# A last gate tile made in two token parts, and a shorter reciprocal root

## The chip, the core and the metric

The kernel runs on one core of a Trainium2 chip. The metric is device time in microseconds (us): the median of several runs, beside one profiled execution whose trace shows every instruction. TensorE multiplies matrices (in the profile PE, its weight loads PEld), VectorE (DVE) and ScalarE (ACT) do elementwise work, GpSimd (POOL) and SyncE (SP) mostly start transfers.

## What is computed

One inference step of a hybrid decoder trunk with one layer: 256 prompt tokens and 8 samples of 4 tokens, 288 tokens in all, of width 2048. The part that matters here is the end of the layer and the norm that is used throughout:

```python
def rmsnorm(x, g):
    xf = x.astype(jnp.float32)
    y = xf * lax.rsqrt(jnp.mean(xf * xf, axis=-1, keepdims=True) + EPS)
    return (y * g.astype(jnp.float32)).astype(x.dtype)
...
    gate = jax.nn.sigmoid(rmsnorm(h, g_pg) @ w_pg)
    h = h + (p_l @ w_ple) * gate
...
    y_prompt = rmsnorm(hp, g_final)
    y_sample = rmsnorm(hs, g_final)
```

Ahead of that stand a combined input projection, a state-space head group, a gated spatial mixing group, an output projection and a feed-forward block, all joined by such norms.

## The kernel before, in words

Activations lie transposed: the 2048 channels are 16 tiles of 128 partitions, and the 288 tokens run along the free dimension. A projection makes one output tile of 128 channels at a time: `mtile` loads two halves of 512 KB of weights on SyncE's queue, `split_w` cuts each into a rounded part (`whi`, ScalarE, L177) and a rest (`wlo`, VectorE, L178), and `mm3` (L184 to L186) multiplies each of 16 blocks three times (hi by hi, hi by lo, lo by hi) in the fp32r type. So an output tile is 48 matmuls with 288 columns each, and every matmul has its own weight load. The splits are given a higher priority than the work around them; otherwise the framework orders each engine's instructions from the program's order and a simulated timeline.

A norm needs one number for each token. `sum_tokens` (L109) sums squares over partitions by three matmuls against a column of ones, each of which shows as two passes; it gives a tile of 128 partitions and 3 columns, one column for tokens 0 to 127, one for 128 to 255 and one for the last 128 (of which only the last 32 tokens are needed). `rsqrt_compact` (L76) turns it into reciprocal roots on VectorE: x, a first guess by integer arithmetic on the bits, three Newton steps. `bcast_tokens` (L121) brings the result back to all partitions by two transposes (L125) and one small matmul (L126). There are eight such norms: `rm` before the first projection, `rg` four times, `rv`, `rf`, `rp`, and `ro` at the end.

The last stage is the loop over 16 output tiles of the gate projection (`w_pg`). For each tile, VectorE multiplies by the norm (L835), ScalarE takes a tanh (L836), VectorE adds and multiplies with the embedding (L837) and adds to `h` (L838), ScalarE squares (`no.add`, L146), VectorE adds to the running sum `sacc` (L147), and ScalarE scales `h` by the final gain (L846). The chain of one tile runs under the matmuls of the next. For the last tile these steps are made in two halves of 128 and 160 tokens, the sums of the tiles ahead are taken early (`part`, L845, six passes between the last matmuls), and the last tile's squares are summed by themselves. After the root and the broadcast, VectorE multiplies `h` in nine pieces of one or two tiles (L851), each followed by its store (L852) on ScalarE's or SyncE's queue in turn.

Of the kernel before, what the change touches and what calls it, by code (L numbers as in the profile page):

```python
# [10 lines left out]
F32 = mybir.dt.float32  # L11
F32R = mybir.dt.float32r
I32 = mybir.dt.int32
AF = mybir.ActivationFunctionType
ALU = mybir.AluOpType
PSUM = bass.MemoryType.PSUM

P = 128
NT = 288
KD = 16  # L20
EPS = 1e-6
# [8 lines left out]
V_MIX, V_FFN, V_PG, V_FIN, V_SSD, V_CM, V_DSK, V_CB, V_CW = 0, 16, 32, 48, 64, 80, 96, 112, 136  # L30
# [10 lines left out]
def hybrid_step(ctx: ExitStack, tc: tile.TileContext, xT, wa, wd, wple, pT, vec, cst, wdt, dtal,  # L41
                sconv, h0T, wsT, wsS, bsP, bsS,
                o_y, o_ssmp, o_conv, o_ssms, o_v):
    nc = tc.nc
# [4 lines left out]
    pa = ctx.enter_context(tc.tile_pool(name="pacc", bufs=3, space=PSUM))  # L49
    pb = ctx.enter_context(tc.tile_pool(name="pbig", bufs=5, space=PSUM))  # L50

    def slab(dt=F32, name="slab", tag="slab"):
        return sp.tile([P, NT], dt, tag=tag, name=name, bufs=SLOTS[tag])

    def big(name="pb"):
        return pb.tile([P, 512], F32, tag="pb", name=name)

    def small(shape, name, bufs=1, dt=F32):
        return cp.tile(shape, dt, tag=name, name=name, bufs=bufs)
# [9 lines left out]
    def bc_mid(ap, n):  # L69

        return ap.unsqueeze(1).to_broadcast([ap.shape[0], n, ap.shape[1]])

    def f32(ap):
        return ap.bitcast(F32)

    def rsqrt_compact(ss, n, eps, name, part=None):  # L76

        x = small([P, 3], name + "x")
        y = small([P, 3], name + "y")
        t = small([P, 3], name + "t")  # L80
        if part is None:
            nc.vector.tensor_scalar(x, ss, 1.0 / n, eps, op0=ALU.mult, op1=ALU.add)
        else:
            nc.vector.scalar_tensor_tensor(x, ss, 1.0 / n, part, op0=ALU.mult, op1=ALU.add)
        nc.vector.tensor_scalar(t.bitcast(I32), x.bitcast(I32), 1, None, op0=ALU.logical_shift_right)  # L85
        nc.vector.tensor_scalar(y.bitcast(I32), t.bitcast(I32), -1, 0x5F3759DF, op0=ALU.mult, op1=ALU.add)  # L86
        for _ in range(3):
            nc.vector.tensor_mul(t, y, y)  # L88
            nc.vector.scalar_tensor_tensor(t, t, -0.5, x, op0=ALU.mult, op1=ALU.mult)  # L89
            nc.vector.scalar_tensor_tensor(y, t, 1.5, y, op0=ALU.add, op1=ALU.mult)  # L90
        return y

    def quads(ap):
# [12 lines left out]
    def sum_tokens(ps, acc, first=True, last=True):  # L106

        for c, t in enumerate((0, P, NT - P)):
            nc.tensor.matmul(ps[:, c:c + 1], lhsT=acc[:, t:t + P], rhs=ones[:, 0:1], start=first and c == 0,  # L109
                             stop=last and c == 2)  # L110

    def sum_compact(acc):

        ps = big()
        sum_tokens(ps, acc)
        return ps[:, 0:3]

    def rstd_compact(acc, n, eps, name, part=None):
        return rsqrt_compact(sum_compact(acc), n, eps, name, part)

    def bcast_tokens(r, keep_psum=False):  # L121

        ps = big()
        for c in range(2):
            nc.tensor.transpose(ps[:, c * P:(c + 1) * P], r[:, c:c + 1].to_broadcast([P, P]), ident)  # L125
        nc.tensor.matmul(ps[:, 256:288], lhsT=r[:, 2:3].to_broadcast([P, P]),  # L126
                         rhs=ident[:, 96:128], start=True, stop=True)
        if keep_psum:
            return ps[:, :NT]
        o = slab(name="rs", tag="rs")  # L130
        nc.scalar.copy(o, ps[:, :NT])
        return o
# [34 lines left out]
    def load(src, k):  # L167
        raw = st.tile([P, 1024], F32, tag="raw", name="raw", bufs=4)
        nc.sync.dma_start(raw[:, :k * P], src.rearrange("p k m -> p (k m)"))
        return raw  # L170

    def split_w(raw, n, to=None, ahead=AHEAD):
        w_hi, w_lo = to or [st.tile([P, 1024], F32R, tag=t, name=t) for t in ("whi", "wlo")]
        a, b = w_hi[:, :n * P], w_lo[:, :n * P]
        r = raw[:, :n * P]
        with tc.high_priority(offset=ahead):
            nc.scalar.copy(a, r)  # L177
            nc.vector.tensor_sub(b, r, f32(a))  # L178
        return w_hi, w_lo

    def mm3(ps, w, k, act, first, last):
        hi, lo = act
        wh, wl = w[0][:, k * P:(k + 1) * P], w[1][:, k * P:(k + 1) * P]
        nc.tensor.matmul(ps, lhsT=wh, rhs=hi, start=first, stop=False)  # L184
        nc.tensor.matmul(ps, lhsT=wh, rhs=lo, start=False, stop=False)  # L185
        nc.tensor.matmul(ps, lhsT=wl, rhs=hi, start=False, stop=last)  # L186
# [18 lines left out]
    ones = small([P, P], "ones")  # L205
    T1, U, ident = (csts[:, c:c + P] for c in (C_T1, C_U, C_I))
# [8 lines left out]
    def vcol(base, i):  # L215
        return vecs[:, base + i:base + i + 1]
# [6 lines left out]
    start = tc.tile_pool(name="start", bufs=1)  # L223
# [33 lines left out]
    for c in range(4):  # L257
        w = split_w(wraw[c], 8)
        for j in range(4):
            ps = pa.tile([P, NT], F32, tag="acc", name="acc")  # L260
# [14 lines left out]
    with tc.high_priority(offset=400):  # L275
        rs0 = bcast_tokens(rstd_compact(sqa[:, 0], 2048.0, EPS, "rm"), keep_psum=True)
# [3 lines left out]
    for k in range(KD):  # L280
        nc.tensor.matmul(pdt[32 * (k % 4):32 * (k % 4) + 32, 0:NT], lhsT=gw[:, k], rhs=xin[k // 2][:, k % 2],
                         start=k < 4, stop=k >= 12, tile_position=(0, 32 * (k % 4)))
# [297 lines left out]
    def y_norm_a(g, grp):  # L580
        return g, rstd_compact(grp.acc, 512.0, 4.0 * EPS, "rg")
# [22 lines left out]
    ss = {}  # L604
# [109 lines left out]
    at = 0  # L714
    for g in range(4):
        tiles = [16 + g, 20 + g] + list(range(4 * g, 4 * g + 4))
        zs = []
        for j, i in enumerate(tiles):
            ps = ps01[at] if at < 3 else mtile(wa[at], n_act)
# [31 lines left out]
    hp, h, mlp_pool, mp, sw = hp_box["pools"]  # L751
    for m in range(KD):
        ps = mtile(wa[40 + m], ycat[:16])
        nc.vector.tensor_add(h[:, m], h[:, m], ps)

    for i in range(nvt, KD):
        ps = mtile(wa[56 + i], n_act)
# [3 lines left out]
    for i in range(KD):  # L761
        ps = mtile(wa[72 + i], n_act)
        us.append(gelu2(ps, hp.tile([P, NT], F32, tag="u", name="u", bufs=4))[0])
        advance(1)
        while us and ss and i - len(us) + 1 in ss:
            k = i - len(us) + 1
# [12 lines left out]
    for m in range(KD):  # L779
        ps = mtile(wa[88 + m], ycat[16:])  # L780
# [6 lines left out]
    g_act = []  # L787
    rs = None
    for half in range(2):
        hid = []  # L790
        for m in range(22):
            mm = 22 * half + m
            pg = mtile(wa[104 + 2 * mm], f_act)
            pu = None
            if rs is None:
                r = rstd_compact(nf.acc, 2048.0, EPS, "rf")
                pu = mtile(wa[105 + 2 * mm], f_act)
                rs = bcast_tokens(r)
            G = hp.tile([P, NT], F32, tag="g2", name="G", bufs=3)
            t, u = slab(name="Gt", tag="ta"), slab(name="Up", tag="td")  # L800
            nc.vector.tensor_mul(G, pg, rs)  # L801
            nc.scalar.activation(t, G, AF.Tanh, scale=0.5)  # L802
            nc.vector.scalar_tensor_tensor(G, t, 1.0, G, op0=ALU.add, op1=ALU.mult)  # L803
            if pu is None:
                pu = mtile(wa[105 + 2 * mm], f_act)
            nc.vector.scalar_tensor_tensor(u, pu, 0.5, rs, op0=ALU.mult, op1=ALU.mult)  # L806
            nc.vector.tensor_mul(u, u, G)  # L807
            hid.append(split(u, make=extra if m >= 18 else None))
        for m in range(KD):
            ps = mtile(wd[half, m], hid)  # L810
            nc.vector.tensor_add(h[:, m], h[:, m], ps)  # L811
            if half == 1:
                g_act.append(split(h[:, m], gain=vcol(V_PG, m), tags=LONG))
                ng.add(h[:, m])
                if m == 7:
                    ple = fp.tile([P, KD, NT], F32, name="ple", bufs=1)
# [3 lines left out]

    no = SumSq()
    wait, rs = [], None
    for m in range(KD):
        wait.append(mtile(wa[192 + m], g_act))
        if m == 0:
            r = rstd_compact(ng.acc, 2048.0, EPS, "rp")
            continue
        if rs is None:
            rs = bcast_tokens(r)
        for k in range(m + 1 - len(wait), m + 1):  # L830
            ps = wait.pop(0)
            G = hp.tile([P, NT], F32, tag="g2", name="G", bufs=3)

            for c in (slice(0, NT),) if k < KD - 1 else (slice(0, P), slice(P, NT)):
                nc.vector.tensor_mul(G[:, c], ps[:, c], rs[:, c])  # L835
                nc.scalar.activation(G[:, c], G[:, c], AF.Tanh, scale=0.5)  # L836
                nc.vector.scalar_tensor_tensor(G[:, c], G[:, c], 1.0, ple[:, k, c], op0=ALU.add, op1=ALU.mult)  # L837
                nc.vector.scalar_tensor_tensor(h[:, k, c], G[:, c], 0.5, h[:, k, c], op0=ALU.mult, op1=ALU.add)  # L838
                if k == KD - 1:
                    nc.scalar.activation(G[:, c], h[:, k, c], AF.Square)  # L840
            if k < KD - 1:
                no.add(h[:, k], scratch=G)
                if k == KD - 2:
                    part = small([P, 3], "part")
                    nc.vector.tensor_scalar(part, sum_compact(no.acc), 1.0 / 2048.0, EPS, op0=ALU.mult, op1=ALU.add)  # L845
            nc.scalar.activation(h[:, k], h[:, k], AF.Identity, scale=vcol(V_FIN, k))  # L846
    rs = bcast_tokens(rstd_compact(G, 2048.0, EPS, "ro", part), keep_psum=True)
    at = 0
    for i, n in enumerate((1, 1, 2, 2, 2, 2, 2, 2, 2)):
        hq = h[:, at:at + n]  # L850
        nc.vector.tensor_mul(hq, hq, bc_mid(rs, n))  # L851
        (nc.sync if i % 2 else nc.scalar).dma_start(o_y[:, at:at + n], hq)  # L852
        at += n


def _consts():
# [104 lines left out]
```

## Time and profile before

| | us |
|---|---|
| median of three runs | 1747.91 (1745.03 to 1748.62) |
| the profiled execution, its own time | 1745.97 |
| its span in the trace | 1744.2 |
| TensorE's mean granted clock in it | 0.991 of full speed |

The page of the profile gives for each engine the busy time and its share of the span. Rows of groups give line, engine, operation, output and inputs, shapes, count, then busy us and mean ns of one. Rows of the timeline give start, length, engine, line and operation; where neighbouring instructions of a group are merged, the count is behind the `x`, and the length is from the first start to the last end. In brackets stands the idle time before, and what ended it. Ends of matmuls are modelled, so the distance between starts says more than the length.

### The profile page before, as it was taken

What the parts mean: (1) busy time and instruction counts of PE and PEld (TensorE: products, weight loads), DVE (VectorE), ACT (ScalarE), POOL (GpSimd) and SP (SyncE); (2) the same over time, 40 slices, a digit from 0 to 9 for tenths busy, and PEclk for the clock granted to TensorE, in tenths of its full rate; (3) what the DMA queues carried; (4) which work ended last, traced back from release to release, by engine and by line L of the source; (5) the groups of instructions that cost most, each with busy time, mean ns of one, the idle gap of its engine ahead of it and who ended that gap; (6) DMA issues with size and microseconds to landing.
All of it is one profiled execution on the core that took longest, in us unless ns stands there. A gap on an engine that the chain in (4) does not pass through costs nothing.

```text
span 1744.2 us, 31331 instructions
## 1 busy us (share of the span) xinstructions
PE 1712.5 (98%) x12920; PEld 1686.5 (97%) x12920; DVE 1067.0 (61%) x1680; ACT 806.3 (46%) x1354; POOL 40.5 (2%) x100
## 2 busy tenths in 40 slices
PE   7999999999999999999999999999999999999996
PEld 6989999989999999999999999999999999999996
DVE  6778888775455876555555554444555555555665
ACT  5677676643356444443333333333333333344453
POOL 2001011010000000000000000000000000000000
PEclk8999999999999999999999999999999999999998
DMA  8447375665555446555455455555555555555552
GB/s 309 165 142 285 128 272 190 222 253 173 164 166 169 153 136 219 171 163 164 164 164 168 160 168 157 167 166 175 162 166 164 164 169 159 163 166 166 170 167 93
DMA packets 86240, 307.00 MB, mean 176 GB/s; under 512 B 9969, under 2 KB 10481, under 8 KB 85329
## 3 DMA queue, kind: packets, MB, share of 16 engines
q1 hardware_dynamic: 77760, 275.07, 48.5%
q0 software_dynamic: 7616, 28.60, 4.3%
q8 instruction: 101, 1.65, 0.4%
q10 hardware_dynamic: 720, 1.33, 0.2%
q14 instruction: 43, 0.34, 0.1%
HBM read 290.18 MB, written 14.79 MB: 175 GB/s over the span
## 4 chain that ended last, share of the span: by engine, by line
PE 76%; DVE 0%; issue 0%; DVEq 0%
PE acc L184 25%; PE acc L186 25%; PE acc L185 25%; PE pb L643 0%; DVE h L851 0%; PE pb L635 0%; PE pb L109 0%; PE pb L125 0%; PE pb L126 0%; DVE rot L89 0%; DVE rot L88 0%; DVE roy L90 0%; DVEq L950 0%; DVE rot L85 0%; DVE roy L86 0%
## 5 line engine op out<-in xcount | busy, mean ns | idle before, releaser
L184 PE MATMUL acc<-hi,whi 128*128 128x288 f32 x4032 | 1195.5, 297 | 5.9 <-ACT whi L177 5.9
L186 PE MATMUL acc<-hi,wlo 128*128 128x288 f32 x4032 | 1189.4, 295 | 3.5 <-DVE wlo L178 3.3
L185 PE MATMUL acc<-lo,whi 128*128 128x288 f32 x4032 | 1191.1, 295 | 0.0
L177 ACT CAST whi<-raw 128x1024 fp32r<-128x1024 f32 (+1 forms) x516 | 534.2, 1036 | 820.3 <-PE acc L185 635.9
L178 DVE TENSOR_TENSOR wlo<-raw,whi 128x1024 fp32r<-128x1024 f32 (+1 forms) x516 | 622.7, 1208 | 469.1 <-ACT whi L177 464.5
L186 PEld LDWEIGHTS acc<-hi,wlo 128*128 128x128 f32 x4032 | 760.0, 189 | 9.1 <-DVE wlo L178 5.4
L184 PEld LDWEIGHTS acc<-hi,whi 128*128 128x128 f32 x4032 | 757.7, 188 | 11.2 <-ACT whi L177 7.0
L185 PEld LDWEIGHTS acc<-lo,whi 128*128 128x128 f32 x4032 | 758.9, 188 | 1.5 <-issue 1.3
L806 DVE SCALAR_TENSOR_TENSOR Up<-acc,rs 128x288 f32<-128x288 f32 x44 | 20.1, 457 | 42.2 <-PE acc L186 42.2
L801 DVE TENSOR_TENSOR G<-acc,rs 128x288 f32<-128x288 f32 x44 | 20.1, 457 | 41.6 <-PE acc L186 41.6
L382 DVE SCALAR_TENSOR_TENSOR cva<-cbuf,cwh,cva 128x312 f32<-128x312 f32 x72 | 38.4, 536 | 0.5
L597 ACT ACTIVATE gt<-gt 128x288 f32<-128x288 f32 x32 | 14.2, 443 | 40.6 <-DVE gt L596 40.6
L429 ACT ACTIVATE xw<-xdt,dec 128x64 f32<-128x64 f32 x96 | 24.7, 338 | 5.2 <-DVE xdt L426 5.1
L411 ACT ACTIVATE M<-cq,cum 128x128 f32<-128x128 f32 x64 | 19.9, 389 | 7.3 <-DMA cq<-cdram 7.2
L460 DVE TENSOR_TENSOR h<-h,pb 128x512 f32<-128x512 f32 x32 | 20.4, 682 | 2.9 <-PE pb L458 2.8
L807 DVE TENSOR_TENSOR Up<-Up,G 128x288 f32<-128x288 f32 x44 | 20.2, 459 | 1.5
L467 DVE TENSOR_TENSOR h<-h,decS 128x512 f32<-128x512 f32 x32 | 20.1, 684 | 0.5 <-PE pb L533 0.5
L803 DVE SCALAR_TENSOR_TENSOR G<-Gt,G 128x288 f32<-128x288 f32 x44 | 19.9, 453 | 0.1
L802 ACT ACTIVATE Gt<-G 128x288 f32<-128x288 f32 x44 | 19.2, 437 | 1.4 <-DVE G L801 1.4
L163 DVE TENSOR_TENSOR lo<-Up,hi 128x288 fp32r<-128x288 f32 x44 | 19.9, 451 | 0.0
L162 ACT CAST hi<-Up 128x288 fp32r<-128x288 f32 x44 | 19.1, 433 | 1.3 <-DVE Up L807 0.5
L811 DVE TENSOR_TENSOR h<-h,acc 128x288 f32<-128x288 f32 x32 | 14.5, 455 | 6.0 <-PE acc L186 6.0
(269 smaller groups left out, 786.4 us busy)
## 6 DMA issues: line engine op xcount, KB each, us to landing
raw<-in_wa_dram SPq DMA_DIRECT2D x416, 512.0 KB, 3.6
raw<-in_wd_dram SPq DMA_DIRECT2D x64, 512.0 KB, 3.5
raw<-in_wd_dram SPq DMA_DIRECT2D x32, 384.0 KB, 3.1
h<-in_h0T_dram POOLq DMA_DIRECT2D x16, 512.0 KB, 8.0
out_dram<-h POOLq DMA_DIRECT2D x16, 512.0 KB, 5.5
cq<-cdram SPq DMA_DIRECT2D x4, 1152.0 KB, 7.3
xin<-in_xT_dram SPq DMA_DIRECT2D x8, 288.0 KB, 6.8
pdram<-ple POOLq DMA_DIRECT2D x16, 144.0 KB, 4.7
```

The source lines that it names most:

```text
L177: nc.scalar.copy(a, r)
L178: nc.vector.tensor_sub(b, r, f32(a))
L184: nc.tensor.matmul(ps, lhsT=wh, rhs=hi, start=first, stop=False)
L185: nc.tensor.matmul(ps, lhsT=wh, rhs=lo, start=False, stop=False)
L186: nc.tensor.matmul(ps, lhsT=wl, rhs=hi, start=False, stop=last)
L382: nc.vector.scalar_tensor_tensor(ao, cb[:, j:j + NCO], wt[j], ao, op0=ALU.mult, op1=ALU.add)
L429: nc.scalar.activation(xw[:, 64 * h:64 * h + 64], xd[:, 64 * h:64 * h + 64], AF.Identity, scale=dec[:, c, 8 * g + h:8 * g + h + 1])
L460: nc.vector.tensor_add(h0[q][:, i], h0[q][:, i], pss[q])
L467: nc.vector.tensor_mul(r3(hh, 64), r3(hh, 64), bc_in(decS[:, 2 * q + i, hs], 64))
L801: nc.vector.tensor_mul(G, pg, rs)
L806: nc.vector.scalar_tensor_tensor(u, pu, 0.5, rs, op0=ALU.mult, op1=ALU.mult)
L807: nc.vector.tensor_mul(u, u, G)
```

## The change

`rsqrt_compact` takes a tile of any width. The first guess takes one instruction instead of two (the halving and the subtraction from the constant are made as one multiplication and addition on the integer value). The three Newton steps become one third-order step of four instructions and one Newton step of three. For a width of one, where x and y are scalars of each partition, both products of a step are one instruction, and the last factor is returned to the caller instead of being multiplied in.

The loop over the gate's tiles stops ahead of the last. The last tile's weights are loaded and split once, and its matmuls are made in two parts, first for tokens 0 to 127, then for 128 to 287, each into its own accumulator: 96 matmuls of 128 or 160 columns instead of 48 of 288. After 11 of the second part's 16 blocks TensorE takes the first part's sums (running sum and the last tile's squares together, one column). The first part's root, broadcast, multiplies and stores come beside the second part: half of them behind the second part's gate, half behind the second part's root. The second part's outputs then go in five pieces of 1, 3, 4, 4 and 4 tiles. `tc.issue_after` puts an engine's instructions behind the one named. `part` is gone.

```diff
-    def rsqrt_compact(ss, n, eps, name, part=None):
-
-        x = small([P, 3], name + "x")
-        y = small([P, 3], name + "y")
-        t = small([P, 3], name + "t")
-        if part is None:
-            nc.vector.tensor_scalar(x, ss, 1.0 / n, eps, op0=ALU.mult, op1=ALU.add)
-        else:
-            nc.vector.scalar_tensor_tensor(x, ss, 1.0 / n, part, op0=ALU.mult, op1=ALU.add)
-        nc.vector.tensor_scalar(t.bitcast(I32), x.bitcast(I32), 1, None, op0=ALU.logical_shift_right)
-        nc.vector.tensor_scalar(y.bitcast(I32), t.bitcast(I32), -1, 0x5F3759DF, op0=ALU.mult, op1=ALU.add)
-        for _ in range(3):
-            nc.vector.tensor_mul(t, y, y)
-            nc.vector.scalar_tensor_tensor(t, t, -0.5, x, op0=ALU.mult, op1=ALU.mult)
-            nc.vector.scalar_tensor_tensor(y, t, 1.5, y, op0=ALU.add, op1=ALU.mult)
+    def rsqrt_compact(ss, n, eps, name):
+
+        w = ss.shape[1]
+        x = small([P, w], name + "x")
+        y = small([P, w], name + "y")
+        t = small([P, w], name + "t")
+        nc.vector.tensor_scalar(x, ss, 1.0 / n, eps, op0=ALU.mult, op1=ALU.add)
+        nc.vector.tensor_scalar(y.bitcast(I32), x.bitcast(I32), -0.5, float(0x5F3759DF), op0=ALU.mult, op1=ALU.add)
+
+        def residual():
+            if w == 1:
+                nc.vector.tensor_scalar(t, y, y, x, op0=ALU.mult, op1=ALU.mult)
+            else:
+                nc.vector.tensor_mul(t, y, y)
+                nc.vector.tensor_mul(t, t, x)
+
+
+        residual()
+        nc.vector.scalar_tensor_tensor(t, t, -10.0 / 3.0, t, op0=ALU.add, op1=ALU.mult)
+        nc.vector.scalar_tensor_tensor(y, t, 5.0, y, op0=ALU.add, op1=ALU.mult)
+        a = -0.5 * (3.0 / 8.0) ** 3
+        if w == 1:
+            residual()
+            nc.vector.tensor_scalar(y, t, 1.5 * 3.0 / 8.0 / a, y, op0=ALU.add, op1=ALU.mult)
+            return y, a
+        nc.vector.tensor_mul(t, y, y)
+        nc.vector.scalar_tensor_tensor(t, t, a, x, op0=ALU.mult, op1=ALU.mult)
+        marks["rsqrt"] = nc.vector.scalar_tensor_tensor(y, t, 1.5 * 3.0 / 8.0, y, op0=ALU.add, op1=ALU.mult)
         return y
...
-    for m in range(KD):
+
+    def gated(k, ps, rs, c, no=None):
+
+        G = hp.tile([P, NT], F32, tag="g2", name="G", bufs=3)
+        nc.vector.tensor_mul(G[:, c], ps[:, c], rs[:, c])
+        nc.scalar.activation(G[:, c], G[:, c], AF.Tanh, scale=0.5)
+        nc.vector.scalar_tensor_tensor(G[:, c], G[:, c], 1.0, ple[:, k, c], op0=ALU.add, op1=ALU.mult)
+        marks["gated"] = nc.vector.scalar_tensor_tensor(h[:, k, c], G[:, c], 0.5, h[:, k, c],
+                                                        op0=ALU.mult, op1=ALU.add)
+        if no is None:
+            nc.scalar.activation(G[:, c], h[:, k, c], AF.Square)
+        else:
+            no.add(h[:, k], scratch=G)
+        nc.scalar.activation(h[:, k, c], h[:, k, c], AF.Identity, scale=vcol(V_FIN, k))
+        return G
+
+    for m in range(KD - 1):
...
-    rs = bcast_tokens(rstd_compact(G, 2048.0, EPS, "ro", part), keep_psum=True)
-    at = 0
-    for i, n in enumerate((1, 1, 2, 2, 2, 2, 2, 2, 2)):
-        hq = h[:, at:at + n]
-        nc.vector.tensor_mul(hq, hq, bc_mid(rs, n))
-        (nc.sync if i % 2 else nc.scalar).dma_start(o_y[:, at:at + n], hq)
-        at += n
+            gated(k, wait.pop(0), rs, slice(0, NT), no)
+
+
+    k = KD - 1
+    w = [split_w(load(wa[192 + k, :, 8 * i:8 * i + 8], 8), 8) for i in range(2)]
+    parts = [slice(0, P), slice(P, NT)]
+    pss = [pa.tile([P, NT], F32, tag="acc", name="acc") for _ in parts]
+    sums = [big() for _ in parts]
+
+    def products(j, ks):
+        c = parts[j]
+        for i in ks:
+            mm3(pss[j][:, c], w[i // 8], i % 8, [x[:, c] for x in g_act[i]], i == 0, i == KD - 1)
+
+    def final_sums(j, G):
+        cols = (0,) if j == 0 else (P, NT - P)
+        for x in (no.acc, G):
+            for i, t in enumerate(cols):
+                mm = nc.tensor.matmul(sums[j][:, i:i + 1], lhsT=x[:, t:t + P], rhs=ones[:, 0:1],
+                                      start=x is no.acc and i == 0, stop=x is G and i == len(cols) - 1)
+        return mm
+
+    def final_rstd(j):
+
+        ro = big()
+        if j == 0:
+            r, scale = rsqrt_compact(sums[j][:, 0:1], 2048.0, EPS, "roa")
+            nc.tensor.transpose(ro[:, 0:P], r.to_broadcast([P, P]), ident)
+            return ro[:, 0:P], scale
+        r = rsqrt_compact(sums[j][:, 0:2], 2048.0, EPS, "rob")
+        nc.tensor.transpose(ro[:, 0:P], r[:, 0:1].to_broadcast([P, P]), ident)
+        nc.tensor.matmul(ro[:, P:160], lhsT=r[:, 1:2].to_broadcast([P, P]), rhs=ident[:, 96:128],
+                         start=True, stop=True)
+        return ro[:, 0:160], None
+
+    def put(j, ro, scale, ns, at=0):
+        for i, m in enumerate(ns):
+            hq = h[:, at:at + m, parts[j]]
+            if scale is None:
+                nc.vector.tensor_mul(hq, hq, bc_mid(ro, m))
+            else:
+                nc.vector.scalar_tensor_tensor(hq, hq, scale, bc_mid(ro, m), op0=ALU.mult, op1=ALU.mult)
+            (nc.sync if j == 0 or i % 2 else nc.scalar).dma_start(o_y[:, at:at + m, parts[j]], hq)
+            at += m
+
+    products(0, range(KD))
+    products(1, range(11))
+    summed = final_sums(0, gated(k, pss[0], rs, parts[0]))
+    with tc.issue_after(summed.ins):
+        products(1, range(11, KD))
+    G = gated(k, pss[1], rs, parts[1])
+    first = final_rstd(0)
+    with tc.issue_after(marks["gated"].ins):
+        put(0, *first, (4, 4))
+    final_sums(1, G)
+    second = final_rstd(1)
+    with tc.issue_after(marks["rsqrt"].ins):
+        put(0, *first, (4, 4), 8)
+    put(1, *second, (1, 3, 4, 4, 4))
```

More of the change, by code (lines that the diff above doesn't have):

```diff
@@ L74, in f32 @@
         return ap.bitcast(F32)
-    def rsqrt_compact(ss, n, eps, name, part=None):
-        x = small([P, 3], name + "x")
-        y = small([P, 3], name + "y")
-        t = small([P, 3], name + "t")
-        if part is None:
-            nc.vector.tensor_scalar(x, ss, 1.0 / n, eps, op0=ALU.mult, op1=ALU.add)
-        else:
-            nc.vector.scalar_tensor_tensor(x, ss, 1.0 / n, part, op0=ALU.mult, op1=ALU.add)
-        nc.vector.tensor_scalar(t.bitcast(I32), x.bitcast(I32), 1, None, op0=ALU.logical_shift_right)
-        nc.vector.tensor_scalar(y.bitcast(I32), t.bitcast(I32), -1, 0x5F3759DF, op0=ALU.mult, op1=ALU.add)
-        for _ in range(3):
-            nc.vector.tensor_mul(t, y, y)
-            nc.vector.scalar_tensor_tensor(t, t, -0.5, x, op0=ALU.mult, op1=ALU.mult)
-            nc.vector.scalar_tensor_tensor(y, t, 1.5, y, op0=ALU.add, op1=ALU.mult)
+    marks = {}
+    def rsqrt_compact(ss, n, eps, name):
[22 more added lines that the diff above has]
+        marks["rsqrt"] = nc.vector.scalar_tensor_tensor(y, t, 1.5 * 3.0 / 8.0, y, op0=ALU.add, op1=ALU.mult)
         return y
@@ L116, in sum_compact, with rstd_compact @@
         return ps[:, 0:3]
-    def rstd_compact(acc, n, eps, name, part=None):
-        return rsqrt_compact(sum_compact(acc), n, eps, name, part)
+    def rstd_compact(acc, n, eps, name):
+        return rsqrt_compact(sum_compact(acc), n, eps, name)
     def bcast_tokens(r, keep_psum=False):
@@ L830, in hybrid_step @@
         for k in range(m + 1 - len(wait), m + 1):
[L831 to L846, printed above, removed]
-    rs = bcast_tokens(rstd_compact(G, 2048.0, EPS, "ro", part), keep_psum=True)
-    at = 0
-    for i, n in enumerate((1, 1, 2, 2, 2, 2, 2, 2, 2)):
-        hq = h[:, at:at + n]
-        nc.vector.tensor_mul(hq, hq, bc_mid(rs, n))
-        (nc.sync if i % 2 else nc.scalar).dma_start(o_y[:, at:at + n], hq)
-        at += n
+            gated(k, wait.pop(0), rs, slice(0, NT), no)
```

## The prediction

> **What bounds the kernel now.** I read the page of the profile first, for the share of each engine, then TensorE's waits, then the timeline of the last 23 us.
>
> ```profile
> span 1744.2 us, 31331 instructions
> PE 1712.5 (98%) x12920; PEld 1686.5 (97%) x12920; DVE 1067.0 (61%) x1680; ACT 806.3 (46%) x1354; POOL 40.5 (2%) x100
> ```
>
> TensorE works for 98% of the span. A change can shorten the run only if TensorE gets less to do, or where TensorE waits, or after its last instruction. The list of its waits shows where it idles on a reciprocal root:
>
> ```profile
> PE pb L125 <- DVE rmy L90: 3.4, 1, 3.4
> PE pb L125 <- DVE roy L90: 2.5, 1, 2.5
> PE pb L109 <- issue: 1.9, 1, 1.9
> ```
>
> Of the eight calls of the root, only the first (`rm`, before the first projection) and the last (`ro`, at the end) hold TensorE up. The other six, four `rg` and `rv`, `rf`, `rp`, are in no row of the list: shortening them is worth nothing, and the cover is the matmul stream that runs meanwhile. The third row is the wait for the last tile's gate and square. The timeline of the end, in which PE is TensorE, DVE VectorE and ACTq a DMA issue on ScalarE's queue:
>
> ```profile
> 1721.47 0.29 PE L184 MATMUL acc<-hi,whi 128*128 128x288 f32 x1
> ...
> 1727.34 0.29 PE L186 MATMUL acc<-hi,wlo 128*128 128x288 f32 x1
> 1727.47 0.72 PE L109 MATMUL pb<-ones,sacc 128*128 128x1 f32 x6
> 1728.06 0.38 PE L184 MATMUL acc<-hi,whi 128*128 128x288 f32 x1
> ...
> 1728.27 0.30 PE L185 MATMUL acc<-lo,whi 128*128 128x288 f32 x1
> 1728.41 0.29 PE L186 MATMUL acc<-hi,wlo 128*128 128x288 f32 x1
> 1728.74 0.52 DVE L835 TENSOR_TENSOR G<-acc,rs 128x128 f32<-128x128 f32 x2 [0.35 <-PE acc L186]
> ...
> 1730.22 0.57 ACT L840 ACTIVATE G<-h 128x128 f32<-128x128 f32 x2 [0.59 <-DVE h L838]
> 1730.63 0.82 PE L109 MATMUL pb<-ones,G 128*128 128x1 f32 x6 [1.93 <-issue]
> 1731.49 0.16 DVE L84 SCALAR_TENSOR_TENSOR rox<-pb,part 128x3 f32<-128x3 f32 x1 [1.06 <-PE pb L109]
> ...
> 1733.66 0.16 DVE L90 SCALAR_TENSOR_TENSOR roy<-rot,roy 128x3 f32<-128x3 f32 x1
> 1733.97 0.66 PE L125 MATMUL pb<-cst,roy 128*128 128x128 f32 x2 [2.51 <-DVE roy L90]
> 1734.42 0.47 PE L126 MATMUL pb<-cst,roy 128*128 128x32 f32 x2
> 1734.93 5.47 DVE L851 TENSOR_TENSOR h<-h,pb 128x288 f32<-128x288 f32 x9 [1.11 <-PE pb L126]
> 1740.43 0.34 ACTq L852 DMA_DIRECT2D out_dram<-h  x1
> ```
>
> The last tile starts at 1721.47 and ends at 1728.41 + 0.29 = 1728.70. From there everything is serial to the end at 1744.20: gate and square to 1730.79, sums to 1731.49, root to 1733.82, broadcast to 1734.93, nine multiplies to 1740.40, then the last store. These 15.5 us are what the change wants to fold into the matmuls. Its price is paid on TensorE, which has no idle time in the last tile.
>
> **The change part by part.** All times are in this profiled execution, whose own time is 1745.97 us: its span of 1744.2 and 1.77 around it.
>
> *Roots.* The chain has 12 instructions before: one for x, two for the first guess, three times three. After it has 9 where w is over 1 (x, guess, four, three) and 7 where w is 1. In `ro` 11 steps lie between the starts at 1731.49 and 1733.66, so a step is 0.197 us and three fewer save 0.59. This counts twice. At the start the chain of `rm` gates this:
>
> ```profile
> 36.45 0.69 PE L125 MATMUL pb<-cst,rmy 128*128 128x128 f32 x2 [3.45 <-DVE rmy L90]
> ...
> 37.34 3.30 PE L281 MATMUL pdt<-xin,gw 128*32 128x288 f32 x32
> 40.56 0.53 PE L184 MATMUL ps<-hi,whi 128*128 128x288 f32 x2
> ```
>
> TensorE goes from the broadcast to the dt matmuls and the first projection without a gap, so all of it moves up: **-0.59**. Late next would be the normalized activations on VectorE, and they start from the same broadcast.
>
> *The last tile's matmuls.* Before, 48 matmuls of 288 columns: from 1721.47 to 1727.34 there are 44 intervals, so one takes 0.133 us and 48 take 6.40. After, there are 96, of 128 and 160 columns, each with its own load of 128x128 weights. No row shows an fp32r matmul below 288 columns. The nearest row with full weight loads and nearly nothing to stream is the six passes of L109 with one column: from 1727.34 to 1728.27 pass one matmul of L186, six passes and one of L184, so a pass takes (0.93 - 0.27)/6 = 0.111. That is the pace of load and issue, and a narrow matmul cannot be paid less than it on this evidence. I take 0.111 for both widths, because by columns alone they would cost less (0.133/288 = 0.463 ns a column, 0.059 and 0.074 us) and so hide under the load. The sums of the running squares shrink from six passes in the tile to four, since the other columns' sums go behind the last matmul. So 7.06 becomes 100 passes x 0.111 = 11.10: **+4.04**. Bounds: by columns alone 48 x 0.133 = 6.4 for both parts, 4.26 less; at the full 0.133 each 2.1 more; at the pace of plain f32 (next fence) 12.9 more.
>
> ```profile
> 594.01 0.61 PE L643 MATMUL pb<-wsr,vt 128*128 128x128 f32 x4
> ...
> L643 PE MATMUL pb<-wsr,vt 128*128 128x128 f32 x64 | 9.6, 274 | 0.0
> ...
> 109.05 1.02 PE L506 MATMUL pb<-xw,btm 128*128 128x512 f32 x2
> ...
> L506 PE MATMUL pb<-xw,btm 128*128 128x512 f32 x8 | 4.1, 593 | 0.0
> ```
>
> A plain f32 matmul shows as two passes. At 128 columns the starts lie (0.61 - 0.274)/3 = 0.112 apart, at 512 columns 1.02 - 0.593 = 0.43, some 0.83 ns a column. Two passes would be 0.224 for 128 columns and 0.267 for 160, together 0.491 x 48 = 23.6.
>
> The Trainium skill, page "TensorE: Matmul & The Clock Gate", section "Back-to-back issue gap", gives about 81 ns for a sustained pair of load and matmul at 128 columns. By it 96 matmuls would be an estimated 7.8 us, and the whole change about 2.2 us faster instead of 0.7 slower. The trace's one-column pairs at 0.111 with f32 weights speak against it here, so the sum goes by the row.
>
> *Gate and square.* Before, two halves through five instructions, 1728.74 to 1730.79, 2.05 us. After the last matmul only the 160 columns are left.
>
> ```profile
> L835 DVE TENSOR_TENSOR G<-acc,rs 128x160 f32<-128x160 f32 x1 | 0.3, 314 | 0.0
> ...
> L840 ACT ACTIVATE G<-h 128x160 f32<-128x160 f32 x1 | 0.3, 336 | 0.0
> ...
> L851 DVE TENSOR_TENSOR h<-h,pb 128x576 f32<-128x576 f32 x7 | 4.7, 747 | 0.0
> L851 DVE TENSOR_TENSOR h<-h,pb 128x288 f32<-128x288 f32 x2 | 0.8, 452 | 1.1 <-PE pb L126 1.1
> ```
>
> Five of 0.31 to 0.34 with four handovers of some 0.03 make 1.75: **-0.30**. The first part's gate runs under the second part's matmuls: it needs some 2 us, the 33 matmuls ahead of its sums take 3.7, so TensorE does not wait.
>
> *First outputs.* Two multiplies of 512 columns sit behind the gate on VectorE, queued ahead of the second root. In the nine multiplies 5.47 = 2 x 0.37 + 6 x 0.664 + 0.747, with 0.37 the step of 288 columns and 0.664 that of 576 (an instruction starts some 0.08 before the one ahead of it ends). At 1.02 ns a column a 512 step is 0.60. From gate to root VectorE had 0.34 + 0.03 + 0.70 = 1.07 free (square, handover, sums); two steps need 1.22, and with a drain I take **+0.2**. The second root saves **-0.59**. Behind it come two more multiplies in the gap of the broadcast, which was 1.11 and shrinks by one transpose: 1.22 against 1.11, **+0.15**. If the first root were not done by then, this would cost more (a rival, below).
>
> *Second outputs.* Widths 160, 480 and three of 640: 0.24 + 0.57 + 2 x 0.73 + 0.81 = 3.08 instead of 5.47: **-2.39**.
>
> *Stores.* They shrink to rows of 512 and 640 bytes from 2304, in 9 DMAs as before, four of them early. SyncE's queue carries the early ones; nothing else waits in it.
>
> ```profile
> out_dram<-h ACTq DMA_DIRECT2D x4, 288.0 KB, 2.3
> ...
> DMA packets 1211, 2.27 MB, mean 391 GB/s; under 512 B 128, under 2 KB 327, under 8 KB 1211
> ```
>
> From 1736.5 to 1742.3 the stores move 2.27 MB at 391 GB/s, so they run at VectorE's pace. The second part, 1.31 MB in 3.08 us, asks for 425 GB/s: **+0.2** of backlog. No row shows short rows at speed. If they cost nothing the term is 0; at 240 GB/s, six tenths of the row, it is about +2.4.
>
> The Trainium skill, page "DMA: Bandwidth & Descriptors", section "Why small descriptors are slow (HBM only)", counts about 3 cycles for each packet beside its 32-byte beats. By it rows of 640 bytes run at an estimated 0.87 of the wire and 2304 at 0.96, which would make the term some 0.6; no run here shows it.
>
> Sum: -0.59 + 4.04 - 0.30 + 0.20 - 0.59 + 0.15 - 2.39 + 0.20 = **+0.7 us**, so 1746.7 for this execution. The median of the runs shown is 1747.91, 1.94 above it, and the same step gives **1748.6**.
>
> **The rivals.** *Narrow matmuls at f32's pace.* In the last tile a narrow fp32r matmul takes the two-pass time, 0.224 and 0.267. For it: every fp32r matmul in the trace has 288 or more columns, and all narrow ones are f32. Against it: each fp32r matmul of the last tile is one instruction, and nothing shows a dependence on width. The sum becomes +13.6, 1761.5: clearly slower. It decides once the mean interval passes 0.140, where the sum reaches 3.5.
>
> *Narrow matmuls paid by columns.* If the loads overlapped fully, 0.059 and 0.074 would give -3.5, 1744.4. For it: TensorE's loads run beside its matmuls, 97% of the span beside 98%. Against it: 0.111 for one column. The same page of the Trainium skill states in its section "Step-by-step: what each phase is for" that throughput is purely the number of columns streamed; the L109 rows do not agree where the stream is one column.
>
> *The first root is late.* If VectorE gets the seven instructions of the first root behind the second gate, 7 x 0.197 + about 1.0 for the broadcast stand ahead of the first outputs and thus of the second root: +2.4, total +3.1, 1751.0. For it: the program writes it in that order. Against it: VectorE's order in the trace follows readiness (the weight splits run ahead of earlier lines), and its inputs are ready 1.7 us of matmuls earlier.
>
> **How the numbers follow.** A measurement of this kernel tells a difference of about 0.2%, 3.5 us, from none. Load-bound matmuls (+0.7; alone from 1747.5 to 1752.0, by 0.133 a pair or slow stores): 0.60. F32's pace: 0.18. By columns: 0.12. Late first root: 0.10. Faster by over 0.2% takes about two thirds of the third case and little else, 0.09. Slower takes the second, four tenths of the fourth and a tenth of the first, 0.28. The rest, 0.63, is the same. The range must reach f32's pace, or more than 2 in 10 would be left out, and it leaves out most of the third case: 1745.0 to 1762.0.
>
> **What would show it.** In the changed profile: narrow matmuls starting 0.11 apart, and the last tile taking 11 us with its four sums; if 0.06 to 0.08 or over 0.2, that term failed. Second root 9 steps of 0.2; first multiply of the second part about 1.3 us behind it; from the last matmul to the end about 12.8 us instead of 15.5. The first projection matmul near 40.0 instead of 40.56. Seven instructions of the first root under the second part's matmuls, not behind its gate. Stores well below 390 GB/s at the end would show short rows.

## The result, and the profile after

The changed kernel takes 1737.98 us (median of 4 runs, 1737.12 to 1739.04) against 1747.53 (1745.03 to 1748.62) for the kernel before on the same chip: ratio 0.9946, 95% interval 0.9934 to 0.9957. It is some 9.5 us faster, where +0.7 was forecast. The profiled execution took 1737.12, so its trace can stand beside that of before (1745.97). The head of its page:

```profile
span 1735.3 us, 31405 instructions
PE 1710.4 (99%) x12968; PEld 1686.8 (97%) x12968; DVE 1064.6 (61%) x1659; ACT 806.1 (46%) x1355; POOL 40.4 (2%) x100
```

TensorE is busy 2.1 us less than before (1712.5), though the last tile has 48 more matmuls. The span is 8.9 us shorter, so most of the gain is idle time that went. To find where, I number the projection matmuls (those of `mm3`) in order of start and take, for the n-th, its start in the trace of before minus its start in the trace of another kernel. This lead, in us, for all kernels of this study, each in its profiled execution (the experiments follow):

| kernel | n = 100 | 400 | 700 | 2220 | 2340 | 12000 |
|---|---|---|---|---|---|---|
| changed kernel | 1.73 | 1.72 | 3.40 | 3.71 | 11.27 | 11.25 |
| all new roots, old last tile | 0.37 | 0.35 | 2.02 | 2.35 | 9.91 | 9.90 |
| old roots, new last tile | -0.36 | -0.37 | -0.77 | -1.64 | -3.14 | -3.16 |
| new root in `rg` alone | 0.16 | 0.15 | -0.13 | -0.40 | 7.14 | 7.16 |
| new root in `rm` alone | 1.17 | 1.15 | 2.82 | 4.24 | 2.92 | 2.91 |
| new root in the last `rg` alone | 0.09 | 0.09 | 0.26 | -0.19 | 2.73 | 2.71 |
| old roots, mask later | -0.48 | -0.50 | -0.79 | -0.46 | 2.71 | 3.03 |
| old roots, `rg` of higher priority | 0.69 | 0.69 | 0.53 | 0.91 | 4.09 | 4.09 |
| changed kernel, long store rows | 0.49 | 0.39 | 2.06 | 2.38 | 9.91 | 9.89 |
| new roots in `rm` and `rg` | 1.50 | 1.50 | 3.17 | 3.49 | 11.03 | 11.05 |

The first row tells three things. The lead is made at three places: before the first projection, between matmuls 400 and 700 (1.68), and above all between 2220 and 2340 (7.56), which in before run from 380 to 404 us. From there it stays, to the last tile. The column n = 100 differs from one execution to the next: two kernels that were profiled twice show 1.73 and 1.00 (the changed one), 0.37 and 1.88 (all new roots, old last tile). Their steps between 2220 and 2340 agree to 0.02. And the last tile, which the change is about, adds nothing to it: from its first matmul to the end of the span it takes 1735.3 - 1710.22 = 25.08 us after and 1744.20 - 1721.47 = 22.73 before, so it loses 2.35.

The windows of before around the big step (columns: length, then busy time of PE, PEld, DVE, ACT and POOL with counts, TensorE's granted clock, DMA share, GB/s):

```profile
385.00:390.00 5.00, 3.63 (x26) 3.13 (x25) 3.25 (x7) 2.96 (x6) 0.00 (x0) 1.00 1.03 419
390.00:395.00 5.00, 4.55 (x34) 4.31 (x33) 2.11 (x6) 1.26 (x3) 0.00 (x0) 1.00 0.85 355
395.00:400.00 5.00, 2.43 (x9) 1.96 (x10) 5.00 (x5) 1.87 (x2) 0.00 (x0) 0.81 0.15 22
400.00:405.00 5.00, 5.00 (x34) 5.00 (x34) 1.75 (x2) 1.05 (x1) 0.00 (x0) 0.85 0.83 278
```

and of after:

```profile
385.00:390.00 5.00, 5.00 (x40) 5.00 (x39) 4.25 (x6) 2.93 (x3) 0.00 (x0) 1.00 1.01 415
390.00:395.00 5.00, 5.00 (x40) 5.00 (x40) 3.06 (x3) 1.43 (x2) 0.00 (x0) 1.00 0.80 317
395.00:400.00 5.00, 5.00 (x40) 5.00 (x40) 3.60 (x4) 1.72 (x2) 0.00 (x0) 1.00 0.43 155
```

Before, TensorE is busy for 2.43 of the 5 us from 395, VectorE for all 5; then the clock falls below 1. After, TensorE runs through. The waits of before between 380 and 402 us (total, times, longest) name the weight splits, `whi` and `wlo`:

```profile
PE acc L184 <- ACT whi L177: 2.5, 3, 1.4
PE acc L186 <- DVE wlo L178: 2.3, 3, 1.2
```

In after the same stretch has no row. Why VectorE was late with the splits stands in its timeline, before

```profile
394.06 1.19 DVE L754 TENSOR_TENSOR h<-h,acc 128x288 f32<-128x288 f32 x3 [2.89 <-PE acc L186]
395.16 2.29 DVE L628 TENSOR_TENSOR wsr<-wsr,cst 128x2048 f32<-128x2048 f32 x1
397.36 3.49 DVE L178 TENSOR_TENSOR wlo<-raw,whi 128x1024 fp32r<-128x1024 f32 x3
```

and after (lines are 15 further down there: L769 is L754, L193 is L178, L643 is L628)

```profile
385.00 0.82 DVE L769 TENSOR_TENSOR h<-h,acc 128x288 f32<-128x288 f32 x2 [0.68 <-PE acc L201]
385.96 2.36 DVE L193 TENSOR_TENSOR wlo<-raw,whi 128x1024 fp32r<-128x1024 f32 x2
388.44 0.46 DVE L769 TENSOR_TENSOR h<-h,acc 128x288 f32<-128x288 f32 x1
389.39 1.23 DVE L193 TENSOR_TENSOR wlo<-raw,whi 128x1024 fp32r<-128x1024 f32 x1 [0.50 <-ACT whi L192]
390.53 2.29 DVE L643 TENSOR_TENSOR wsr<-wsr,cst 128x2048 f32<-128x2048 f32 x1
```

Before, three output tiles of the out-projection end together (three additions to `h` in a row), then a mask multiply of 2.29 us, which is for the spatial group and not needed yet, stands in VectorE's queue ahead of three splits for which TensorE waits. After, additions and splits alternate and the mask multiply comes behind the splits. The lines of this code are the same in both kernels. What differs is the order that the framework gave them, on TensorE as well: counted in the traces, the sums of the last `rg` stand behind 2216 projection matmuls before and behind 2206 after, its broadcast behind 2256 before and 2232 after.

### The profile page after: what moved, and what is told of

The parts are those of the page before. It is cut to its first block, busy times and chain, and to the rows that moved or that the text cites. A ratio compares the mean times of both kernels' runs of the same rounds, so it can differ in the third digit from the quotient of the medians.

```text
span 1735.3 us, 31405 instructions
## 1 busy us (share of the span) xinstructions
PE 1710.4 (99%) x12968; PEld 1686.8 (97%) x12968; DVE 1064.6 (61%) x1659; ACT 806.1 (46%) x1355; POOL 40.4 (2%) x100
## 4 chain that ended last, share of the span: by engine, by line
PE 98%; DVE 1%; DMA 0%; ACT 0%; issue 0%; SPq 0%; DVEq 0%; ACTq 0%
PE acc L199 31%; PE acc L201 31%; PE acc L200 31%; PE pb L456 1%; PE pb L548 0%; PE pb L658 0%; DMA raw<-in_wple_dram 0%; PE pb L473 0%; DVE wlo L193 0%; PE pb L439 0%; PE pb L124 0%; PE ps L199 0%; PE ps L201 0%; PE ps L200 0%; PE pb L650 0%
## 5 line engine op out<-in xcount | busy, mean ns | idle before, releaser
L199 PE MATMUL acc<-hi,whi 128*128 128x288 f32 (+1 forms) x4048 | 1198.5, 296 | 4.5 <-ACT whi L192 4.5
L200 PE MATMUL acc<-lo,whi 128*128 128x288 f32 (+1 forms) x4048 | 1193.6, 295 | 0.0
L201 PE MATMUL acc<-hi,wlo 128*128 128x288 f32 (+1 forms) x4048 | 1190.7, 295 | 0.6 <-DVE wlo L193 0.6
L193 DVE TENSOR_TENSOR wlo<-raw,whi 128x1024 fp32r<-128x1024 f32 (+1 forms) x516 | 622.9, 1209 | 468.9 <-ACT whi L192 465.9
L178 DVE TENSOR_TENSOR lo<-Up,hi 128x288 fp32r<-128x288 f32 x44 | 19.9, 451 | 0.0
```

## The experiments

Four theories. A: the shorter roots make the whole gain by way of the order, and the two-part tile loses. B: the two-part tile makes it. C: a root counts only where TensorE waits for it (`rm`, `ro`), which was the prediction's. D: any shift in the simulated order breaks the stall up.

**One part of the change at a time.** In the first kernel every norm gets the new nine-instruction chain and the last tile stays in one part; in the second it is the other way round.

```diff
--- before
+++ all new roots, old last tile
+        if True:
+            nc.vector.tensor_scalar(y.bitcast(I32), x.bitcast(I32), -0.5, float(0x5F3759DF), op0=ALU.mult, op1=ALU.add)
...
+            nc.vector.scalar_tensor_tensor(y, t, 1.5 * 3.0 / 8.0, y, op0=ALU.add, op1=ALU.mult)
+            return y
--- after
+++ old roots, new last tile
+        if name[:2] != "ro":
...
+            for _ in range(3):
...
+            return y
```

> The kernel before with the nine-instruction root in all eight norms and the old last tile and outputs. Theory A (the roots give everything: they reorder the instructions ahead of the out-projection, and the two-part tile by itself loses 2.4 us): the last tile starts 11 us earlier as in the changed kernel, the end keeps its 22.7 us less 0.6, so about 11.8 us faster than before, 1736, and faster than the changed kernel by some 2 to 3 us. Theory B (the two-part tile gives the gain): within 2 us of before, 1745 to 1747. The stall near 395 us in the trace of before is gone by A and there by B.

Measured 1736.01 us (1734.60 to 1736.75), ratio to before 0.9935 [0.9921, 0.9950].

> The changed kernel with the old twelve-instruction root in the first and the six middle norms; the last tile's roots stay new. Theory A: the stall near 395 us and the one ahead of it are back, the last tile starts near 1721.5 as before and the part behind it is 2.4 us longer: about 1750, slower than before by 2 to 2.5 us. Theory B: 1738 to 1741.

Measured 1750.72 us (1747.06 to 1752.34), ratio 1.0019 [1.0009, 1.0028]. The roots alone make the whole gain, and the two-part tile alone makes nothing better: A, against B. In the second kernel the stall at 380 to 404 us is there, and 1.5 us worse than in before (table), so its loss is not the tile's alone. TensorE's waits in it are those of before (2.5 and 2.3); what is longer is the low clock behind them, 0.97, 0.50 and 0.85 in the three windows from 395 to 410 us.

**Which root.** The same edit under a condition on the norm's name.

```diff
--- before
+++ new root in rg alone
+        if name == "rg":
...
+            return y
--- before
+++ new root in rm alone
+        if name == "rm":
...
+            return y
```

> The kernel before with the nine-instruction root in the four rg norms alone, which no wait of TensorE in the trace of before names. Theory A: they remove the stalls near 130 and near 395 us, 9 of the 11.3 us by which the last tile is earlier, so about 1738 to 1739. Theory C (roots count only where TensorE waits on them, so rm and ro): within 0.5 us of before, 1747.

Measured 1739.66 us (1738.81 to 1740.66), ratio 0.9957 [0.9943, 0.9972]: C falls. The four `rg` are in no row of TensorE's waits, and shortening them brings 7.54 of lead between matmuls 2220 and 2340, as the whole change does (7.56). The part that was expected near 130 us does not come with it: between 400 and 700 the lead falls by 0.28, and the time stays above the expected 1739.

> The kernel before with the nine-instruction root in the first norm alone. Theory A: the order of VectorE's instructions around the out-projection stays that of before, so the stall near 395 us stays; only the start moves up, by 0.6 (three instructions) to 1.7 us (what the changed kernel shows there): 1745.5 to 1747. Theory D (any shift of the simulated timeline breaks up the stall, so which root is shortened does not matter): about 1740 or less.

Measured 1744.16 us (1742.98 to 1745.89), ratio 0.9983 [0.9973, 0.9992]: D falls, since here the order shifts too (between 400 and 700) and the stall stays (lead -1.32 in that step). Its waits are those of before, 2.5 and 2.3. It is worse because the clock stays low for longer:

```profile
390.00:395.00 5.00, 1.97 (x9) 1.26 (x8) 5.00 (x6) 2.63 (x3) 0.00 (x0) 0.84 0.10 39
395.00:400.00 5.00, 5.00 (x23) 5.00 (x22) 1.61 (x2) 0.16 (x1) 0.00 (x0) 0.50 0.77 237
```

With 0.98 in the next window that is (0.16 + 0.50 + 0.02) x 5 = 3.4 us of clock, against (0.19 + 0.15) x 5 = 1.7 in before. Against C speaks that `rm` brings 1.67 more between matmuls 400 and 700, well behind the place where TensorE waits for it. With it, and with 1.42 more between 700 and 2220 that nothing here explains, the time is below the 1745.5 that was expected at least.

**Length or order.** A shorter root in the last group makes the last tile of `ycat` (the out-projection's input) ready earlier by 0.6 us, and it can change the order. The next three kernels part the two. In the first only the last group's root is short. The other two keep the old root everywhere and change only the order (`last_v` is the last instruction of the last tile that feeds the spatial group).

```diff
--- before
+++ new root in the last rg alone
-        return g, rstd_compact(grp.acc, 512.0, 4.0 * EPS, "rg")
+        return g, rstd_compact(grp.acc, 512.0, 4.0 * EPS, "rg3" if g == 3 else "rg")
...
+        if name == "rg3":
...
+            return y
--- before
+++ old roots, mask later
...
-        nc.vector.tensor_mul(w, w, bc_mid(T1, KD))
+        with tc.issue_after(last_v):
+            nc.vector.tensor_mul(w, w, bc_mid(T1, KD))
--- before
+++ old roots, rg of higher priority
-        return g, rstd_compact(grp.acc, 512.0, 4.0 * EPS, "rg")
+        with tc.high_priority(offset=400):
+            return g, rstd_compact(grp.acc, 512.0, 4.0 * EPS, "rg")
```

> The kernel before with the new nine-instruction root only in the rg of the last group of gate norms (one root of eight). In it the 2.29 us mask multiply still stands ahead of weight splits in VectorE's order, though behind one more of them than before. Theory 'the length of the last group's root decides' (the last transposes come earlier, so TensorE never runs out): as e3, about 1739.5 us (1738.5 to 1741), no half clock near 390 us, lag +7 at matmul 2340. Theory 'the order of the mask multiply and the splits decides': the stall goes only in part, 1742.5 to 1745.5 us. Theory 'only the start and the tail count' (the prediction's): 1747.

Measured 1745.57 us (1742.95 to 1746.71), ratio 0.9988 [0.9979, 0.9997]: 0.07 above the range for order and 6 above what the length of the last root should give, so that length is not what decides. The step is 2.92 here, and the kernel differs from before by more than one shorter root: the three additions to `h` alternate with the splits, though the mask multiply still stands ahead of them. The clock falls here too, to 0.90 and 0.76 in the windows from 385 to 395 us:

```profile
385.00:390.00 5.00, 3.09 (x19) 2.48 (x18) 3.47 (x7) 3.05 (x6) 0.00 (x0) 0.90 1.04 418
```

> The kernel before with its old twelve-instruction roots, and only the 2.29 us mask multiply (wsr by the mask constant) put behind the last v tile in the order of instructions. Theory 'the order of the mask multiply and the splits decides': the wait for the weight splits near 396 to 399 us goes, and the half clock of 3.4 us behind it: 1742.5 to 1745 us (minus 2.3 for the multiply to minus 5 with the half clock). Theory 'the length of the roots decides, the mask is beside it': 1747.

Measured 1742.87 us (1741.94 to 1745.74), ratio 0.9977 [0.9968, 0.9987].

> The kernel before with its old twelve-instruction roots everywhere, and only a higher priority for the four rg roots in the order of instructions; the mask multiply then stands behind the weight splits, as in e1 and e3. Theory 'order decides': 1740 to 1744 us, no half clock near 390 us. Theory 'the number of instructions in the root decides': 1747.

Measured 1742.61 us (1741.89 to 1743.45), ratio 0.9975 [0.9966, 0.9985]. Both kernels have twelve-instruction roots and are 4 us faster: the order by itself moves the time. VectorE's timeline with the mask later:

```profile
394.57 1.18 DVE L757 TENSOR_TENSOR h<-h,acc 128x288 f32<-128x288 f32 x3 [2.94 <-PE acc L186]
395.67 3.49 DVE L178 TENSOR_TENSOR wlo<-raw,whi 128x1024 fp32r<-128x1024 f32 x3
```

and TensorE's waits there between 380 and 402 us:

```profile
PE acc L186 <- DVE wlo L178: 2.0, 3, 0.9
PE acc L184 <- ACT whi L177: 1.1, 2, 0.6
```

The waits fall from 2.5 + 2.3 = 4.8 to 3.1, and the granted clock, 0.81 and 0.85 in the two windows from 395 to 405 us of before, is 1.00 in both here: at five us each, 0.19 and 0.15 are worth 1.7. Together 3.4, against a step of the lead of 3.17. The step is 3.18 in the kernel with higher priority. So the mask multiply ahead of the splits, with the half clock that followed the idle time, costs 3.2 of the 7.5. The other 4.3 stay in both kernels, and in both the three additions to `h` still stand in a row. With the mask later, the distances between TensorE's starts, less its pace of 0.133, put 1.7 of them on two waits at 394.8 and 395.8 us, behind these three additions, and 2.2 on three waits between 382 and 388, around the root of the last group and right behind it; the last 0.4 is a slower pace. In before that root and its broadcast stand so:

```profile
380.92 0.16 DVE L88 TENSOR_TENSOR rgt<-rgy 128x3 f32<-128x3 f32 x1
381.31 1.23 DVE L178 TENSOR_TENSOR wlo<-raw,whi 128x1024 fp32r<-128x1024 f32 x1 [0.23 <-ACT whi L177]
382.46 0.15 DVE L89 SCALAR_TENSOR_TENSOR rgt<-rgt,rgx 128x3 f32<-128x3 f32 x1
...
385.61 0.38 PE L125 MATMUL pb<-cst,rgy 128*128 128x128 f32 x2
```

A split stands inside the root, and TensorE takes the broadcast behind 2256 projection matmuls. In every kernel with a step of 7.5 the root is in one piece and the broadcast stands behind 2232. In the others the broadcast stands behind 2254 to 2256, also where the four roots have the higher priority, though there the root is in one piece too. So the full gain goes along with the earlier place of the broadcast on TensorE. No kernel moved the broadcast alone: that the 4.3 come from there is argued, not shown. The same holds for why a chain of nine instead of twelve brings the framework to the better order.

**The stores.** In the changed kernel the outputs of each part are written side by side into another buffer and stored as long rows, on the buffer's side as well as in memory; the output array then holds the two parts one after the other in memory.

```diff
+            n = (P, NT - P)[j]
+            row = slice(KD * P * j + at * n, KD * P * j + (at + m) * n)
+            o = ple.rearrange("p a b -> p (a b)")[:, row]
-                nc.vector.tensor_mul(hq, hq, bc_mid(ro, m))
+                nc.vector.tensor_mul(r3(o, n), hq, bc_mid(ro, m))
...
-            (nc.sync if j == 0 or i % 2 else nc.scalar).dma_start(o_y[:, at:at + m, parts[j]], hq)
+            (nc.sync if j == 0 or i % 2 else nc.scalar).dma_start(o_y.rearrange("p a b -> p (a b)")[:, row], o)
```

> The changed kernel, with the outputs of the last gate tile's two parts stored as long contiguous rows instead of rows of 512 and 640 bytes: the multiplies write them side by side in a buffer of their own, and the output array holds the last 288 columns' parts one after the other (the same values in another order in memory). Theory 'short rows slow the last stores': landing goes from 3.6 to 4.0 us back to 2.4 to 2.7, last multiply to span end from 5.3 us to 3.8 to 4.2: 1736.5 us (1736.0 to 1737.0). Theory 'row length is nothing, the stores are limited by being issued late together': 1738 as the changed kernel.

Measured 1737.00 us (1736.76 to 1738.10), ratio 0.9945 [0.9929, 0.9962]; beside the changed kernel's 1737.98 too near to call by the medians. The transfers tell it apart. After, from 1724 us to the end:

```profile
DMA packets 4240, 2.36 MB, mean 209 GB/s; under 512 B 144, under 2 KB 4240, under 8 KB 4240
...
out_dram<-h ACTq DMA_DIRECT2D x2, 320.0 KB, 3.6
out_dram<-h SPq DMA_DIRECT2D x1, 320.0 KB, 4.0
```

and with long rows:

```profile
DMA packets 1296, 2.36 MB, mean 207 GB/s; under 512 B 144, under 2 KB 400, under 8 KB 1296
...
out_dram<-ple ACTq DMA_DIRECT2D x2, 320.0 KB, 2.5
out_dram<-ple SPq DMA_DIRECT2D x1, 320.0 KB, 2.5
```

The same bytes go in 1296 packets instead of 4240, and a 320 KB store lands in 2.5 us instead of 3.6 to 4.0. The last multiply ends at 1731.35 and the span at 1735.3, 3.95 behind it, where the changed kernel has 5.31 (1729.99 to 1735.3). The short rows cost 1.36. The spans are equal because this execution started later: its lead at the last tile is 9.89 against 11.25.

**Side by side.** Five rounds on one chip: new roots in `rm` and `rg` only; all new roots and the old last tile again; the changed kernel again.

> The kernel before with the new nine-instruction root in rm and the four rg only, the old root in rp, rf, rv and ro, the last tile in one part. Theory 'rm and rg make the whole gain, each by itself' (rm: minus 2.9 us of lag before the out-projection, rg: minus 7.5 in it): lag about 10 us after matmul 2340 as in the kernel with all eight, 1736 to 1737.5 us. Theory 'the gain of all eight is not the sum of these two': 1739 us or more.

Measured 1735.30 us (1734.92 to 1735.93), ratio 0.9932 [0.9920, 0.9945]: `rm` and `rg` make the whole gain, 0.7 more than the range expected, and the step at 2220 to 2340 is 7.54.

> The kernel with the nine-instruction root in all eight norms and the last tile in one part once more, side by side with the changed kernel on one chip. Theory A (the two-part tile by itself loses): 1735.5 to 1736.5 us, 1.5 to 2.5 us under the changed kernel. Theory B (the two-part tile is worth nothing or more): the two within 1 us.

Measured 1735.23 us (1734.36 to 1735.87), ratio 0.9931 [0.9919, 0.9943].

> The changed kernel once more beside the one with all the new roots and the last tile in one part: 1737.5 to 1738.5 us; by theory A 1.5 to 2.5 us over that one, by theory B within 1 us of it.

Measured 1737.95 us (1737.83 to 1738.81), ratio 0.9949 [0.9935, 0.9962]. The ranges of these two do not touch: the two-part tile costs 2.7 us beside the same roots, a little over the 2.5 expected at most. The best version of this study is the one without it, 0.9931 of before, and the five shorter roots of `rm` and `rg` are enough for that.

## Why the prediction was wrong, point by point

**The step that failed.** "The other six, four `rg` and `rv`, `rf`, `rp`, are in no row of the list: shortening them is worth nothing, and the cover is the matmul stream that runs meanwhile." For their latency that may hold. But three instructions fewer in `rg` changed the order of VectorE's and TensorE's queues, and the stall at 380 to 404 us, worth 7.5, went with it. Order alone is shown for 3.2 of the 7.5; for the rest it is argued. The trace of before showed the stall, in two rows of the same list of waits that the prediction passed over:

```profile
PE acc L184 <- ACT whi L177: 5.9, 4, 3.4
PE acc L186 <- DVE wlo L178: 3.3, 6, 1.2
```

These 9.2 us, 4.8 of them between 380 and 402 us, are more than the waits of both roots together (5.9). With them in view, a rival "the order falls otherwise and the stall goes" would have had a place, and some -6.5 a price: the 4.8 of waits and the 1.7 of clock behind them. Whether it would come true could not be read from the trace: with the new root in `rm` alone and with the new last tile alone the same waits stay.

**The start.** Forecast -0.59. TensorE's wait for `rmy` falls from 3.4 to 2.9, as forecast:

```profile
PE pb L140 <- DVE rmy L105: 2.9, 1, 2.9
```

From the first instruction of the chain to the broadcast it takes 36.45 - 33.04 = 3.41 before and 34.74 - 31.92 = 2.82 after, which is the -0.59:

```profile
33.04 0.16 DVE L82 TENSOR_SCALAR rmx<-pb 128x3 f32<-128x3 f32 x1 [0.40 <-PE pb L109]
```

```profile
31.92 0.16 DVE L84 TENSOR_SCALAR rmx<-pb 128x3 f32<-128x3 f32 x1
34.74 0.69 PE L140 MATMUL pb<-cst,rmy 128*128 128x128 f32 x2 [2.85 <-DVE rmy L105]
```

The other 1.1 of the lead of 1.73 at the 100th matmul is the chain's earlier start, 31.92 instead of 33.04. No shortened root stands ahead of it, and it varies between executions with old roots (31.91 to 33.40) as with new (31.45 to 32.60). What `rm` brought besides is 1.67 to 1.68 between matmuls 400 and 700, in each of the seven executions with the new root in `rm` and in none of the five others (-0.40 to 0.17). There the small matmuls of the state-space group lie otherwise among the projection's. Why they cost less so is not settled.

**The last tile.** Forecast +1.31 without the start's -0.59; measured +2.35. The timeline of after, from the tile's first matmul:

```profile
1710.22 0.22 PE L199 MATMUL acc<-hi,whi 128*128 128x128 f32 x1
...
1715.42 0.28 PE L201 MATMUL acc<-hi,wlo 128*128 128x128 f32 x1
...
1719.63 0.32 PE L199 MATMUL acc<-hi,whi 128*128 128x160 f32 x1
...
1721.24 0.28 PE L201 MATMUL acc<-hi,wlo 128*128 128x160 f32 x1
```

```profile
1719.81 0.16 DVE L84 TENSOR_SCALAR roax<-pb 128x1 f32<-128x1 f32 x1 [2.79 <-PE pb L880]
...
1721.55 0.33 DVE L842 TENSOR_TENSOR G<-acc,rs 128x160 f32<-128x160 f32 x1
...
1724.08 0.15 DVE L84 TENSOR_SCALAR robx<-pb 128x2 f32<-128x2 f32 x1
...
1725.64 0.16 DVE L105 SCALAR_TENSOR_TENSOR roby<-robt,roby 128x2 f32<-128x2 f32 x1
1725.72 1.28 DVE L903 SCALAR_TENSOR_TENSOR h<-h,pb 128x512 f32<-128x512 f32 x2
1726.92 3.07 DVE L901 TENSOR_TENSOR h<-h,pb 128x160 f32<-128x160 f32 x5
```

- *Narrow matmuls:* the first part's 48 start within 5.20 us, 47 intervals of 0.111; the last 15 of the second part within 1.61, 14 of 0.115. The tile goes from 1710.22 to 1721.24 + 0.28, 11.30, against 7.23 before: +4.07, forecast +4.04. The rivals of f32's pace and of paying by columns are out. The Trainium skill, page "TensorE: Matmul & The Clock Gate", section "Back-to-back issue gap", gives about 81 ns for a pair at 128 columns; this trace does not agree.
- *Gate, square and first outputs:* from the last matmul's end to the second root 2.56, before 2.79: -0.23, forecast -0.30 + 0.20.
- *First root:* it runs at 1719.81 to 1721.40, under the matmuls. The rival of a late first root is out.
- *Second root and gap:* nine steps from 1724.08 to 1725.80, 1.72 against 2.33: -0.61, forecast -0.59. The gap behind it 1.12 against 1.11, forecast +0.15.
- *Second outputs:* 3.07 instead of 5.47: -2.40, forecast -2.39.
- *Stores:* 5.31 behind the last multiply instead of 3.80: **+1.51, forecast +0.2**. This is the mis-sized term. Its upper bound of 2.4 held it; the value was taken near the rate of 2304-byte rows, though the rows shrank to a quarter. The Trainium skill's count of 3 cycles for each packet (page "DMA: Bandwidth & Descriptors", section "Why small descriptors are slow (HBM only)"), by which the term was an estimated 0.6, fell short as well.

The sum of the measured terms, 4.07 - 0.23 - 0.61 + 0.01 - 2.40 + 1.51, is the 2.35. So the tile was read nearly right, with the sign of its cost, and the run's outcome was made 1330 us earlier, where the prediction had put nothing.

## What to carry to other kernels

Where a framework orders the queues by a simulated timeline, an edit off the critical path is not free of effect: look in the list of waits for stalls that hang on the order of a queue, and keep a rival for their going and their coming. Compare two traces by the start of the n-th matmul before believing any story about where the time came from: here it showed at once that the edited place lost time. And split a change of two parts on the chip, since the part that was meant as an aside made all of the gain.

## What the runs showed of the hardware

- An fp32r matmul with its own 128x128 weight load starts 0.11 us behind the last at 128 and 160 columns, 0.133 at 288. The narrowest is only a sixth cheaper than the widest.
- Stores of 320 KB in rows of 640 bytes took 3.6 to 4.0 us to land, with long rows 2.5. Over the same bytes that, with the rows of 512 bytes, cost 1.36 us at the end of the run.
- Short waits in the middle of the run lowered TensorE's granted clock, with no wait longer than 1.4 us. Where TensorE was busy for 3.09 of 5 us (the last `rg` alone) or 2.43 (before), the clock fell in that window and the next, and 1.7 us of clock went; at 1.97 (`rm` alone) it was 3.4, with 0.50 over a whole window. At 3.63 (before, 385 to 390 us) it stayed at 1.00.
